# A two-layer hybrid block: the second layer's in-projection without the context columns of three query blocks

## The chip, the cores and the metric

One core of a Trainium2 chip runs the whole program in one launch. The metric is the device time of that launch in microseconds. Engines: TensorE (PE; its weight loads are PEld), VectorE (DVE), ScalarE (ACT), GpSimd (POOL), and SyncE (SP), which here issues all data transfers.

## What is computed

The reference runs two layers over 1024 latent tokens and 256 context tokens of width 1024. Each layer normalises and modulates the tokens, projects them into the columns of four mixers (two attentions, a state-space model, a long convolution called hyena), runs the mixers, gates them, and projects back. The second layer returns only latent tokens:

```python
for l in range(DEPTH):
    need_ctx = l < DEPTH - 1
    p_l = h_l @ w_in[l]
    p_c = h_c @ w_in[l]
    a_l, a_c = mla_mixer(p_l[..., :o1], p_c[..., :o1], ..., need_ctx)
    g_l, g_c = gqa_mixer(p_l[..., o1:o2], p_c[..., o1:o2], ..., need_ctx)
```

In both attentions the context tokens give keys and values in either layer, `k_c, v_c = keys(p_ctx, False)`. They give queries only where `need_ctx` holds: `o_c = attend(p_ctx, k_c, v_c, False) if need_ctx else None`. So in the second layer the query columns of the context tokens are read by nothing.

## The kernel before

The normalised tokens of a layer lie in SBUF as `hh` and `hl`, the high and low parts of 8 tiles of 128 features by 1280 tokens (1024 latent, then 256 context). The in-projection goes by blocks of 128 output columns. `inproj_cols` (L468) loads a block's weights as `wraw`, splits them into `whi` (ACT, L459) and `wlo` (POOL), and goes over the tokens in chunks: the first of 512, the next of `step`. A chunk is 24 matmuls into one PSUM tile `ipc`: 8 feature tiles, each as `hh` by `whi`, `hl` by `whi` and `hh` by `wlo` (`mm3`, recorded at L224). A `sink` then takes the chunk out of PSUM.

`inproj_qkv` (L492) does this for the seven blocks of the attentions, always over 1280 tokens. Blocks 0 and 1 are the queries of the grouped attention, 2 its keys, 3 its values. Block 4 and the lower half of block 6 are the compressed queries of the latent attention, block 5 its compressed keys and values, and the upper half of block 6 the rotary key. Blocks other than 3 have an entry in `SUMS` (L490): for them the sink also squares the chunk (`sq`), and after the second and the third chunk PE multiplies the squares with a selector `bsel`, 128 tokens at a time. DVE copies these sums of squares into the tile `rs` (128 tokens by 10 token tiles by 8 columns; L518). Block 6 adds its own to those of block 4 there. With `step` 384 the chunks of such a block are 512, 384 and 384.

`prep` (L1384) turns the projected blocks into queries, keys and values in DRAM, in five chunks of 256 tokens, the last the context. It begins with `rs`: DVE adds `eps`, POOL raises the 128x80 tile to the power -1/2 (L1414, tile `nhalf`), DVE negates it into `nrs`. For each chunk it loads `px` and `py` from `qkvD`, transposes `rs` (`prt`), spreads it (`pbc`), rotates (`pR`), and multiplies up (`mv`, `mkn`, `mqn`, `mqr`). `need_q` is false for the context chunk of the second layer.

A layer's program order is in the table `SCRIPT` (L1819). For the second layer it is `Whhuuhqqqqqqqhhh`: W builds the hyena filters (`hps`, `hfilt`, `fdft`, `kt`) and the state-space tables (`pwt`, `sT`, `sF`, `etp`, `kfp`), h projects a hyena block, u a state-space block, q an attention block. After it come, at high priority, hyena (`hyx`, `ldft`, `lX`, `dd`, `ds`, `lU`, `lout`), the state-space scans (`sU`, `sD`, `sV`, `cm`), `prep`, and the finishing stage `ssm_finish` (L1317; `sgy`, `sgg`, `sz`, `sglu`). Then come the projections of the eight gate blocks (`inproj_gate`, `ipt`), attention (`aq`, `kst`, `aS`) and the output projection. The instruction order on each engine is set by a scheduler at build time, from priorities and its own estimate of durations; each engine then runs its queue in order.

Of the kernel before, what the change touches and what calls it, by code (L numbers as in the profile page):

```python
# [187 lines left out]
class K:  # L188
# [300 lines left out]

    SUMS = {0: (128, 0, 2, 0), 1: (128, 0, 2, 2), 2: (128, 2, 2, 4), 4: (128, 4, 1, 6), 6: (64, 4, 1, 6), 5: (128, 5, 1, 7)}  # L490

    def inproj_qkv(self, l, blk, P):  # L492

        late = []

        def sink(ps, c0, m):
            o = P.tile([128, 512], F32, tag="ipo", name="ipo", bufs=3)
            self.nc.scalar.copy(o[:, :m], ps[:, :m])
            self.store(self.qkvD[:, blk, c0:c0 + m], o[:, :m])
            if blk not in self.SUMS:  # L500
                return
            r, s, k, d = self.SUMS[blk]
            sq = P.tile([128, 512], F32, tag="ipo", name="sq", bufs=3)
            self.act(sq[:r, :m], ps[:r, :m], AF.Square)
            late.extend((sq, t) for t in range(m // 128))
            if m == 512:
                return
            nt = len(late)
            q = ps[:, 384:384 + nt * k].rearrange("p (t k) -> p t k", k=k)
            for i, (sq, t) in enumerate(late):  # L510
                self.mm(q[:, i], sq[:r, t * 128:t * 128 + 128], self.bsel[:r, s:s + k], i == 0, i == nt - 1)
            late.clear()
            i1 = (c0 + m) // 128
            dst = self.rs[:, i1 - nt:i1, d:d + k]
            if blk == 6:
                self.tt(dst, q, dst, ADD)
            else:
                self.nc.vector.tensor_copy(dst, q)  # L518

        self.inproj_cols(self.A["w_qkv"][l, blk], 1280, sink, 384 if blk in self.SUMS else 512)  # L520

    def inproj_gate(self, l, g, n, P):

# [860 lines left out]
    def prep(self, l, W, nq):  # L1384


        nc, A = self.nc, self.A
# [29 lines left out]
        for c0, n in self.CHUNKS:  # L1417
            c = slice(c0, c0 + n)
            i0, nt = c0 // 128, n // 128
            lat, need_q = c0 < 1024, c0 < nq  # L1420
            p0 = 0 if need_q else 2
            x = W.tile([128, 7, 256], F32, tag="px", name="px")
            self.load(x[:, p0:6], self.qkvD[:, p0:6, c])
            if need_q:
                for h in range(2):
                    self.load(x[h * 64:h * 64 + 64, 6], self.qkvD[0:64, 6, c])
# [377 lines left out]
def weave(*gens):  # L1804

    out = [None] * len(gens)
    live = dict(enumerate(gens))
    while live:
        for i, g in list(live.items()):
            try:  # L1810
                next(g)
            except StopIteration as e:
                out[i] = e.value
                del live[i]
    return out
# [7 lines left out]
def dit_kernel(ctx: ExitStack, tc: tile.TileContext, A, out):  # L1823
    k = K(tc, A, out)
    k.setup(ctx)
    nc = tc.nc
# [3 lines left out]
    for l in range(2):  # L1830
        need = l == 0
        n = 1280 if need else 1024
# [17 lines left out]
        with k.pool("fil", side="right") as F, k.pool("pol") as Q:  # L1850
            fil = k.filters(l, F, need)
            next(fil)
            mr = ExitStack()
            if l == 0:
                M = mr.enter_context(k.pool("mod"))
                with tc.high_priority(20000):
                    k.mod_setup(M)
                    scl, shf = k.modulation(0, M)
            with k.pool("polt") as P, tc.high_priority(20000):
                poles = k.ssm_poles(l, P, Q)  # L1860
            if l == 0:
                with tc.high_priority(20000), k.pool("np") as P:
                    for g0 in range(0, 10, 2):
                        xns = []
                        for i in (g0, g0 + 1):
                            xt = P.tile([128, 1024], F32, tag="xt", name="xt", bufs=2)
                            k.load_x(xt, i)
                            xn = P.tile([128, 1024], F32, tag="xn", name="xn", bufs=3)
                            k.xn_tile(P, xt, xn, xn)
                            xns.append(xn)  # L1870
                        k.norm_cols(P, (g0, g0 + 1), xns, scl, shf, k.hh, k.hl, 3)
            mr.close()
            tr = ExitStack()
            gens = {"f": fil, "t": k.ssm_tables(l, tr.enter_context(k.pool("tab")), poles)}
            done = {}
            k.rs = k.cp.tile([128, 10, 8], F32, tag="rs", name="rs")

            def step(c):
                if c in done:
                    return False  # L1880
                try:
                    next(gens[c])
                except StopIteration as e:
                    done[c] = e.value
                    tr.close() if c == "t" else None
                return True

            def scan():
                with k.pool("ssm") as Q:
                    weave(k.ssm(l, Q, uD, yD, done["t"], need))  # L1890

            blocks = dict.fromkeys("uqh", 0)
            for c in SCRIPT[l]:
                if c in blocks:
                    x = blocks[c]
                    blocks[c] += 1
                if c == "u":
                    k.inproj_raw(A["w_col"][l, x], 1280, uD[:, x], k.wp)
                elif c == "q":
                    k.inproj_qkv(l, x, k.wp)  # L1900
                elif c == "h":
                    k.inproj_raw(A["w_col"][l, 2 + x], n, hyD[:, x], k.wp)
                elif c in "ft":
                    step(c)
                elif c in "FT":
                    while step(c.lower()):
                        pass
                elif c == "W":
                    while step("f") | step("t"):
                        pass  # L1910
            kf = done["f"]
# [94 lines left out]
```

## Time and profile before

| | |
|---|---|
| median of 3 runs | 2175.04 us (2175.00, 2175.04, 2179.42) |
| the profiled execution | 2180.56 us, its span 2178.8 us |
| mean granted TensorE clock | 0.932 |
| PE, PEld, DVE busy | 89%, 74%, 73% |
| ACT, POOL busy | 42%, 46% |
| second layer: first projection matmul | 1218.22 us |
| second layer: first attention scores | 1789.41 us |

The span is counted from the first to the last instruction, and what lies around it is 1.76 us. Busy shares are averages over stages: the second layer's in-projection, with the filters, scans and preparation woven into it, fills 1218 to about 1790 us, attention 1790 to about 2060, the output projection the rest.

### The profile page before, as it was taken

How to read it: one execution, taken by the hardware profiler on the slowest of the kernel's cores; microseconds unless marked ns; L12 is line 12 of the kernel's file. 1: busy time of each engine (PE TensorE's matmuls, PEld its weight loads, DVE VectorE, ACT ScalarE, POOL GpSimd, SP SyncE). 2: the span in 40 equal slices, each digit the busy share in tenths (PEclk: the TensorE clock that was granted, in tenths of full speed). 3: DMA queues.
4: the chain of work that ended last, by engine and by line, in shares of the span. 5: the costliest groups of instructions: out<-in, count | busy, mean ns of one | idle time of the engine just before them, and what ended most of it. 6: DMA issues, size and time to landing. Idle time of an engine off the chain costs nothing.

```text
span 2178.8 us, 31556 instructions
## 1 busy us (share of the span) xinstructions
PE 1941.8 (89%) x10811; PEld 1615.2 (74%) x10811; DVE 1591.4 (73%) x2985; ACT 917.5 (42%) x1958; POOL 1000.7 (46%) x798
## 2 busy tenths in 40 slices
PE   5788998789899899999998898988888989999988
PEld 1577788678677777788776777888766667899866
DVE  7799528963986588788644398479768878999821
ACT  4422224223333376677523322334223227788611
POOL 4756325664752144434156549236565624240033
PEclk8698898999999999999899998999899999999999
DMA  6422455345766545553243433364456675561063
GB/s 205 133 79 105 148 169 163 102 121 176 228 194 211 170 124 139 161 141 96 80 153 116 129 108 120 125 225 143 129 160 204 209 219 145 141 168 55 11 184 125
DMA packets 261279, 316.55 MB, mean 145 GB/s; under 512 B 46670, under 2 KB 203598, under 8 KB 257792
## 3 DMA queue, kind: packets, MB, share of 16 engines
q1 hardware_dynamic: 261120, 314.55, 47.4%
q8 instruction: 85, 1.39, 0.3%
q14 instruction: 74, 0.61, 0.1%
HBM read 207.61 MB, written 106.86 MB: 144 GB/s over the span
## 4 chain that ended last, share of the span: by engine, by line
PE 44%; DVE 29%; DMA 10%; issue 7%; POOL 4%; ACT 3%; SPq 2%; POOLq 0%; DVEq 0%; ACTq 0%
PE ipc L224 8%; PE apo L224 7%; PE ops L224 6%; PE apt L253 6%; PE aS L224 6%; DVE lU L233 3%; DVE sD L233 3%; SPq L201 2%; DVE sp L233 2%; PE acx L224 2%; PE fdft L224 2%; PE mps L224 1%; DVE lX L233 1%; PE hps L224 1%; DMA px<-qkvD 1%
## 5 line engine op out<-in xcount | busy, mean ns | idle before, releaser
L224 PE MATMUL ipc<-hh,whi 128*128 128x512 f32 (+2 forms) x992 | 386.9, 390 | 24.3 <-DVE rs L518 9.6
L224 PE MATMUL ipc<-hh,wlo 128*128 128x512 f32 (+2 forms) x992 | 380.9, 384 | 3.5 <-POOL wlo L233 3.5
L224 PE MATMUL ipc<-hl,whi 128*128 128x512 f32 (+2 forms) x992 | 381.9, 385 | 1.6 <-POOL hl L233 1.6
L224 PEld LDWEIGHTS ipc<-hh,whi 128*128 128x128 f32 x992 | 196.8, 198 | 59.5 <-DVE rs L518 11.2
L1669 ACT CAST aPh<-apt 128x512 fp32r<-128x512 f32 x328 | 186.6, 590 | 124.3 <-PE apt L253 115.7
L233 DVE TENSOR_TENSOR aPl<-apt,aPh 128x512 fp32r<-128x512 f32 x328 | 223.8, 683 | 20.2 <-ACT aPh L1669 16.0
L233 POOL TENSOR_TENSOR wlo<-wraw,whi 128x512 fp32r<-128x512 f32 x108 | 164.3, 1527 | 154.6 <-ACT whi L459 144.0
L224 PEld LDWEIGHTS ipc<-hh,wlo 128*128 128x128 f32 x992 | 196.5, 198 | 34.8 <-POOL wlo L233 4.3
L224 PEld LDWEIGHTS ipc<-hl,whi 128*128 128x128 f32 x992 | 197.0, 199 | 32.9 <-issue 3.6
L253 PE MATMUL apt<-ident,aP 128*128 128x128 f32 x1312 | 190.0, 275 | 1.5 <-DVE aPl L233 1.0
L1634 DVE TENSOR_REDUCE am<-aS 128x1 f32<-128x1024 f32 x128 | 155.5, 1215 | 13.5 <-PE aS L224 13.5
L224 PE MATMUL aS<-kst,aq 128*128 128x512 f32 x512 | 153.3, 422 | 11.7 <-DMA aq<-gP 6.8
L246 ACT ACTIVATE aP<-aS,am,rs 128x1024 f32<-128x1024 f32 x128 | 155.7, 1217 | 15.3 <-DVE am L243 14.2
L253 PEld LDWEIGHTS apt<-ident,aP 128*128 128x128 f32 x1312 | 148.1, 140 | 16.8 <-DVE aPl L233 6.9
L1697 POOL COPY aLB<-am 128x128 f32<-128x128 f32 x72 | 21.2, 294 | 299.6 <-DVE am L1689 294.0
L224 PE MATMUL apo<-aPh,vst 128*128 128x256 f32 x656 | 138.0, 307 | 15.6 <-ACT aPh L1669 9.1
L224 PE MATMUL apo<-aPl,vst 128*128 128x256 f32 x656 | 123.3, 285 | 3.1 <-DVE aPl L233 3.1
L224 PEld LDWEIGHTS apo<-aPh,vst 128*128 128x128 f32 x656 | 96.0, 190 | 31.0 <-DVE aob L233 15.9
L459 ACT CAST whi<-wraw 128x512 fp32r<-128x512 f32 x124 | 75.5, 618 | 92.7 <-PE ipc L224 48.9
L224 PE MATMUL ops<-owh,omh 128*128 128x512 f32 x288 | 94.2, 408 | 16.4 <-ACT omh L1782 10.3
L224 PEld LDWEIGHTS aS<-kst,aq 128*128 128x128 f32 x512 | 88.7, 193 | 26.8 <-ACT aP L246 7.4
L224 PEld LDWEIGHTS apo<-aPl,vst 128*128 128x128 f32 x656 | 100.1, 189 | 10.0 <-DVE aPl L233 5.3
(368 smaller groups left out, 4490.4 us busy)
## 6 DMA issues: line engine op xcount, KB each, us to landing
wraw<-in_w_col_dram SPq DMA_DIRECT2D x64, 256.0 KB
mraw<-in_w_mod_dram SPq DMA_DIRECT2D x32, 512.0 KB
kst<-mK SPq DMA_DIRECT2D x16, 640.0 KB
omx<-mixD SPq DMA_DIRECT2D x18, 512.0 KB
ogt<-gD SPq DMA_DIRECT2D x18, 512.0 KB
wraw<-in_w_mod_dram SPq DMA_DIRECT2D x32, 256.0 KB
k<-kt SPq DMA_DIRECT2D x16, 512.0 KB
lk<-k SPq DMA_DIRECT2D x8, 1024.0 KB
```

Source lines behind the costliest of these rows:

```text
L201: return self.nc.sync.dma_start(out=out, in_=in_)
L224: self.keep(self.nc.tensor.matmul(out, lhsT, rhs, start=start, stop=stop))
L233: self.keep((eng or self.nc.vector).tensor_tensor(out=out, in0=a, in1=b, op=op))
L246: self.keep(self.nc.scalar.activation(out=out, in_=in_, func=func, **k))
L253: self.keep(self.nc.tensor.transpose(out, in_, self.ident[:p, :p]))
L459: self.nc.scalar.copy(hi, raw)
L1634: self.keep(nc.vector.tensor_reduce(out=x["m"][:, 2 + qi:3 + qi], in_=x["S"][qi], axis=AX.X, op=ALU.max))
L1669: self.keep(nc.scalar.copy(h, ps))
L1697: self.keep(nc.gpsimd.tensor_copy(x["LB"][:, :, o:o + 64], x["m"][:, 10:12].unsqueeze(2).to_broadcast([128, 2, 64])))
```

## The change

`inproj_qkv` is given the layer's number of token columns `n` (1280 in the first layer, 1024 in the second) and uses it for blocks 0, 1 and 4. In the second layer these are projected over the 1024 latent tokens, in chunks of 512, 256 and 256. Blocks 2, 3, 5 and 6 keep 1280 tokens. The context entries of `rs` that the three blocks no longer fill are set by a memset to 1.0 ahead of the projection. `prep` loads the context chunk's `px` in two pieces, without block 4. The first layer's code stays as it was.

```diff
-    def inproj_qkv(self, l, blk, P):
+    def inproj_qkv(self, l, blk, n, P):
         late = []
+        n = n if blk in (0, 1, 4) else 1280
...
-        self.inproj_cols(self.A["w_qkv"][l, blk], 1280, sink, 384 if blk in self.SUMS else 512)
+        self.inproj_cols(self.A["w_qkv"][l, blk], n, sink, (384 if n == 1280 else 256) if blk in self.SUMS else 512)
...
             x = W.tile([128, 7, 256], F32, tag="px", name="px")
-            self.load(x[:, p0:6], self.qkvD[:, p0:6, c])
+            for p in (slice(0, 6),) if need_q else (slice(2, 4), slice(5, 6)):
+                self.load(x[:, p], self.qkvD[:, p, c])
...
             k.rs = k.cp.tile([128, 10, 8], F32, tag="rs", name="rs")
+            if not need:
+                nc.vector.memset(k.rs, 1.0)
...
-                    k.inproj_qkv(l, x, k.wp)
+                    k.inproj_qkv(l, x, n, k.wp)
```

The scheduler orders the second layer anew with these sizes. Three places of the new order matter here.

On PE, from hyena's `lout` transforms to the last sums of squares of block 6 (`ldft` are hyena's next transforms, `gv` the first work of prep; between the rows stand projection matmuls). Before:

```order
L224 MATMUL lout<-lX,hfi 128x128 x12
...
L224 MATMUL ldft<-hyt,hff 128x128 x8
L224 MATMUL ipc<-bsel,sq 128x1 x7
...
L224 MATMUL ipc<-hl,whi 128x384
L224 MATMUL ipc<-hh,whi 128x512
...
L224 MATMUL ipc<-bsel,sq 128x1 x3
L253 MATMUL gv<-ident,px 128x128 x2
```

Now:

```order
L224 MATMUL lout<-lX,hfi 128x128 x12
...
L224 MATMUL ipc<-hh,wlo 128x384
L224 MATMUL ldft<-hyt,hff 128x128 x8
L224 MATMUL ipc<-hh,whi 128x512
...
L224 MATMUL ipc<-bsel,sq 128x1 x2
L224 MATMUL ldft<-hyt,hff 128x128 x8
L224 MATMUL ipc<-bsel,sq 128x1
L224 MATMUL ipc<-hl,whi 128x512
```

Between `lout` and the last `bsel` there stood 26 projection matmuls of 384 columns and 24 of 512; now there are 4 and 16.

On DVE, the adds of block 6's sums into `rs`, the add of `eps`, and what of hyena and prep stands around them. Before:

```order
L233 TENSOR_TENSOR hyt<-lout,hyt 128x512 x2
L233 TENSOR_TENSOR rs<-ipc,rs 128x7
L233 TENSOR_TENSOR ds<-lX 128x1024
L233 TENSOR_TENSOR lX<-ds 128x2x256 x2
L233 TENSOR_TENSOR lU<-lX 128x2x128 x4
L233 TENSOR_TENSOR sp<-px,sp 128x256 x2
...
L236 SCALAR_TENSOR_TENSOR py<-py,gqk,prg 128x256 x2
L233 TENSOR_TENSOR rs<-ipc,rs 128x3
L233 TENSOR_TENSOR rs<-rs,eps 128x80
...
L241 TENSOR_SCALAR nrs<-rs 128x80
```

Now:

```order
L233 TENSOR_TENSOR hyt<-lout,hyt 128x512 x2
L233 TENSOR_TENSOR rs<-ipc,rs 128x7
L233 TENSOR_TENSOR rs<-ipc,rs 128x3
L233 TENSOR_TENSOR rs<-rs,eps 128x80
L233 TENSOR_TENSOR ds<-lX 128x1024
L233 TENSOR_TENSOR lX<-ds 128x2x256 x2
L233 TENSOR_TENSOR lU<-lX 128x2x128 x4
L233 TENSOR_TENSOR sp<-px,sp 128x256 x2
...
L236 SCALAR_TENSOR_TENSOR py<-py,gqk,prg 128x256 x2
L241 TENSOR_SCALAR nrs<-rs 128x80
```

The second add and the `eps` add have moved from behind `py` to ahead of `ds`.

On POOL, the power of `rs` (`rs<-rs,nhalf`), with hyena's `dd`, `lX`, `lU` and `ds` and prep's weight splits `uq`, `ukvl`. Before:

```order
L233 TENSOR_TENSOR dd<-lX 128x1024
L233 TENSOR_TENSOR uq0l<-swr,uq0h 128x512
L233 TENSOR_TENSOR wlo<-wraw,whi 128x512
L233 TENSOR_TENSOR lX<-dd 128x2x128 x4
...
L233 TENSOR_TENSOR lU<-lX 128x2x128
L233 TENSOR_TENSOR rs<-rs,nhalf 128x80
...
L233 TENSOR_TENSOR lX<-lX 128x2x128
...
L233 TENSOR_TENSOR ds<-lU,lk 128x1024
```

Now:

```order
L233 TENSOR_TENSOR dd<-lX 128x1024
L233 TENSOR_TENSOR rs<-rs,nhalf 128x80
L233 TENSOR_TENSOR uq0l<-swr,uq0h 128x512
...
L233 TENSOR_TENSOR lX<-dd 128x2x128 x4
L233 TENSOR_TENSOR wlo<-wraw,whi 128x512
...
L233 TENSOR_TENSOR lU<-lX 128x2x128
...
L233 TENSOR_TENSOR lX<-lX 128x2x128
...
L233 TENSOR_TENSOR ds<-lU,lk 128x1024
```

The power has moved from behind hyena's first `lU` to right behind `dd`, ahead of `uq0l` and `lX`.

## Rows read from the trace of the kernel before

**Rows 1.** The page's table of busy time (share of the span), instructions.

```profile
PE 1941.8 (89%) x10811; PEld 1615.2 (74%) x10811; DVE 1591.4 (73%) x2985; ACT 917.5 (42%) x1958; POOL 1000.7 (46%) x798
```

**Rows 2.** Windows: length; busy PE, PEld, DVE, ACT, POOL; PE clock; DMA share; GB/s.

```profile
1320.00:1340.00 20.00, 19.02 (x88) 15.71 (x89) 16.68 (x22) 3.28 (x6) 18.77 (x11) 0.66 0.30 111
...
1380.00:1400.00 20.00, 20.00 (x141) 17.48 (x140) 11.26 (x34) 6.72 (x18) 3.33 (x3) 1.00 0.20 79
1400.00:1420.00 20.00, 20.00 (x154) 19.12 (x153) 5.37 (x21) 6.87 (x16) 4.95 (x6) 1.00 0.43 113
...
1500.00:1520.00 20.00, 13.87 (x63) 12.94 (x62) 19.88 (x24) 4.30 (x12) 15.97 (x14) 0.74 0.27 86
```

**Rows 3.** The chain that ended last, end of the filters: start, us, what.

```profile
1414.15 7.14 PE fdft L224 x64
1421.69 5.28 DMA k<-kt
```

**Rows 4.** Timeline of PE, end of the attention blocks: start, us, instruction.

```profile
1547.56 3.03 PE L224 MATMUL lout<-lX,hfi 128*128 128x128 f32 x24
...
1557.62 1.95 PE L224 MATMUL ldft<-hyt,hff 128*128 128x128 f32 x16
...
1566.34 0.83 PE L224 MATMUL ipc<-bsel,sq 64*128 64x1 f32 x6
```

**Rows 5.** Timeline of POOL around the power of `rs`.

```profile
1560.27 3.46 POOL L233 TENSOR_TENSOR dd<-lX 128x1024 f32<-128x1024 f32 x1 [5.12 <-ACT lX L803]
1563.69 1.29 POOL L233 TENSOR_TENSOR uq0l<-swr,uq0h 128x512 fp32r<-128x512 f32 x1
...
1566.63 3.81 POOL L233 TENSOR_TENSOR lX<-dd 128x256 f32<-128x256 f32 x4
...
1576.51 0.73 POOL L233 TENSOR_TENSOR lU<-lX 128x256 f32<-128x256 f32 x1
1577.20 13.16 POOL L233 TENSOR_TENSOR rs<-rs,nhalf 128x80 f32<-128x80 f32 x1
...
1594.21 2.42 POOL L233 TENSOR_TENSOR ds<-lU,lk 128x1024 f32<-128x1024 f32 x1 [0.69 <-DVE lU L236]
```

**Rows 6.** Timeline of DVE there; in brackets idle time and what ended it.

```profile
1560.23 1.23 DVE L233 TENSOR_TENSOR ds<-lX 128x1024 f32<-128x1024 f32 x1 [3.05 <-ACT lX L803]
...
1575.88 0.15 DVE L233 TENSOR_TENSOR rs<-ipc,rs 128x3 f32<-128x3 f32 x1
1576.07 0.58 DVE L233 TENSOR_TENSOR rs<-rs,eps 128x80 f32<-128x80 f32 x1
...
1590.39 1.26 DVE L241 TENSOR_SCALAR nrs<-rs 128x80 f32<-128x80 f32 x1 [12.10 <-POOL rs L233]
```

**Rows 7.** Windows, one from preparation to attention, columns as in rows 2.

```profile
1600.00:1800.00 200.00, 167.62 (x786) 128.69 (x785) 162.46 (x240) 62.86 (x145) 100.21 (x77) 0.93 0.71 214
```

**Rows 8.** Timeline of PE: first and last of 71, 24 and 38 projection matmuls.

```profile
1237.94 0.39 PE L224 MATMUL ipc<-hl,whi 128*128 128x512 f32 x1
...
1254.20 0.40 PE L224 MATMUL ipc<-hh,wlo 128*128 128x512 f32 x1
...
1260.88 0.28 PE L224 MATMUL ipc<-hh,whi 128*128 128x256 f32 x1
...
1263.61 0.28 PE L224 MATMUL ipc<-hh,wlo 128*128 128x256 f32 x1
...
1427.78 0.34 PE L224 MATMUL ipc<-hh,wlo 128*128 128x384 f32 x1
...
1434.29 0.34 PE L224 MATMUL ipc<-hh,whi 128*128 128x384 f32 x1
```

**Rows 9.** Timeline of SP's queue: the issue of one of prep's loads.

```profile
1651.89 0.62 SPq L201 DMA_DIRECT2D px<-qkvD  x1
```

**Rows 10.** Timeline of PE, the finishing stage ahead of attention.

```profile
1785.62 3.75 PE L224 MATMUL sglu<-sz,sgw 128*128 128x256 f32 x8 [3.83 <-ACT ipt L246]
...
1795.91 3.78 PE L224 MATMUL sglu<-sz,sgw 128*128 128x256 f32 x8 [4.45 <-DVE sz L236]
```

## The prediction

> **What bounds the kernel now.** I read the page's table of engines first [rows 1]. TensorE (PE) is busy 89% of the span and VectorE (DVE) 73%, which alone says only that neither can be ignored. The edit lies in layer 1's in-projection, so next come the windows of that stretch [rows 2]. Before 1340 us both engines are loaded. From 1380 to 1420 PE is busy 20.00 of 20 us at full granted clock while DVE is busy 11.26 and 5.37: there PE alone sets the pace, and the chain of work that ended last runs through it, ending in 7.14 us of filter transforms and the DMA `k<-kt` behind them [rows 3]. From 1500 to 1520 it is the other way round: DVE 19.88 of 20, PE 13.87 at a granted clock of 0.74. Removing columns pays in the first kind of window and not in the second.
>
> The third place to see is the hinge from in-projection to attention preparation. The last sums of squares end on PE at about 1567 [rows 4]. DVE adds them only at 1575.88, because it runs in order and first does hyena work and the rotary products. GpSimd (POOL) then takes 13.16 us for the power -1/2 of the 128x80 tile `rs`, from 1577.20 to 1590.36 [rows 5], and DVE idles 12.10 us for it at `nrs` [rows 6]. After that, from 1600 to 1800, DVE is busy 162.46 of 200 us, 0.81 [rows 7]; nothing there is saturated, but every dependent step has to get through DVE's queue.
>
> **The change, part by part.**
> *Columns.* Blocks 0, 1 and 4 go from chunks 512+384+384 to 512+256+256. The number of matmuls stays; 48 per block lose 128 columns each, 144 in all. Steady spacing, start to start [rows 8]: 512 columns (1254.20-1237.94)/70 = 0.232 us, 384 columns (1434.29-1427.78)/37 = 0.176, 256 columns (1263.61-1260.88)/23 = 0.119. So each saves 0.057 us, a block 2.7 us, all three 8.2 us of PE time at full clock. The spacing is proportional to columns, about 0.46 ns a column: the weight loads hide even behind 256. The Trainium skill (TensorE: Matmul & The Clock Gate, Back-to-back issue gap) says that in streams of load and matmul pairs the spacing is 81 ns at 128 columns and 131 at 512, set by both operations. By an estimate from that page, 128 columns would be worth 17 ns and the change 2.4 us of PE time in place of 8.2; the rows of this kernel differ, and they decide.
>
> *Blocks 0 and 1* stand on PE ahead of the filter transforms. By the order, the transforms that end at 1421 had 96 chunks' matmuls of 384 columns and 72 of 512 before them since the same point of the queue, and now have 96 of 256 and 80 of 512. That is 96 x 0.057 = 5.5 us less and 8 x 0.232 = 1.9 us more, 3.6 us net at best. Half of the saving (block 0, 2.7 us) falls before 1350, where DVE is loaded too (16.68 of 20 us busy while PE has 19.02 [rows 2]), so I count half of that: 5.5 - 1.35 - 1.9 = **2.2 us** earlier, bounds 0 and 3.6.
>
> *Block 4's* 2.7 us lie in the stretch where DVE is full. I count nothing for them there, since PE's idle time behind DVE covers them; without that cover they would be worth their 2.7 us. They only let the projection run ahead of the scans, which leads to the next term.
>
> *The hinge.* In the new order, between the start of hyena's `lout` transforms and the last sums PE has 4 projection matmuls of 384 columns and 16 of 512, where before it had 26 and 24. That is 22 x 0.176 + 8 x 0.232 = 5.7 us less. The last sums, at 1566.34 + 0.83 = 1567.2 [rows 4], would end at 1561.5. DVE's queue has moved as well: both adds and the eps add now stand right behind `hyt`, ahead of `ds`, `lX`, `lU` and the rotary products. So `rs` is ready about 0.7 us after the sums, at 1562.2. POOL's queue has the power right behind `dd`, which ends at 1560.27 + 3.46 = 1563.7 [rows 5]. The power then starts at 1563.7, not 1577.2: **13.5 us** earlier, and prep's first chunk with it.
>
> What of this is kept? Hyena does not gain: in POOL's new order `uq0l`, the four `lX` and the rest that ran from 1563.69 to 1577.20 now come behind the power, so hyena's `ds`, at 1594.21 before, stays about where it was (13.5 earlier, 13.5 more ahead of it). What is regained is DVE's idle time: the 12.10 us wait at `nrs` is now filled by `ds` to `py`, which took from 1560.23 to 1575.88 [rows 6]. They start at 1562.2 rather than 1560.23 (1.9 us lost, waiting for the sums) and end near 1576, and the power ends at 1576.9, so about 1 us of wait is left. 12.1 - 1.9 - 1.0 = 9.2 us of DVE time. In the stretch that must absorb it DVE is 0.81 busy [rows 7], so I count 9.2 x 0.81 = **7.5 us**. Bounds: 0 if attention waits for hyena alone, 13.5 if it waits for prep alone. I take a value between, nearer to the row of DVE's idle time, since both chains share DVE.
>
> *Small parts.* A 128x80 memset of `rs` is added on DVE, early in layer 1, long before the first sums: between 0.1 us and the 0.58 us of the eps add of the same shape [rows 6], hidden while the filters run. The context chunk's load becomes two DMAs for one: one more issue, 0.62 us of the SP queue for such a load [rows 9], with its chunk long projected. Evictions, squares and stores of 12 chunks shrink on ACT, which is 42% busy [rows 1]: nothing. Fewer sums: 8 tiles for 10 in three blocks, inside the numbers above.
>
> *The tail.* Before, `sglu` of the finishing state-space stage waited 3.83 us for a gate's `ipt` and 4.45 us for `sz` [rows 10]. In the new order all gates' matmuls stand ahead of the last `lout`. The first wait may go (gain up to 4 us), or the gates may hold up `lout`, with the same price the other way. I take 0.
>
> **Sum:** 2.2 + 7.5 = 9.7 us. The profiled execution took 2180.56 us, so 2170.9 for its like; the median of the runs shown is 2175.04, 5.5 us below that execution, so 2165.3 as the prediction. The three runs lie within 4.4 us, and 0.2% (4.35 us) is about what a measurement of this kernel can tell from no change.
>
> **The rivals.**
> *Hidden.* The end is set by hyena on DVE, whose work does not change, and prep's head start is lost again among its waits. For it: DVE full before 1540, and hyena's `ds` not moving in my own sum. Against: the 12.10 us in which DVE stands idle cannot survive the new order. The gain is then 0 to 4 us; with half of the 2.2 us, 2174. Chance 0.19. The Trainium skill (Perfetto Trace Analysis, Identifying the Most-Contended Engine) warns that matmul busy time is a poor measure of TensorE's load and gives weight-load busy time instead. That page would lean to this rival, and here weight loading is busy 74% [rows 1]; the full windows between 1380 and 1420 with matmuls back to back are the evidence against it.
>
> *Slower: hyena behind the power.* The power's new place in POOL's queue delays `lX`, `lU` and `ds` of hyena by those 13.5 us of moved work. It breaks even only if the power starts 13.5 us earlier. If the last sums are late on PE (the second `ldft`, which waits for `hyt`, stands ahead of the last of them), each microsecond missing there comes onto hyena. Should the power gain under 7 us, hyena ends 6.5 us later, less 2.2: 4.3 us slower, past 0.2%. If it gains nothing, 13.5 - 2.2 = 11.3 us, 2186. For it: POOL is in order and hyena's last transforms are among the last things before attention. Against: 5.7 us less stands ahead of the sums. Chance 0.13.
>
> *PE sets everything.* If PE is what attention waits for, the whole 8.2 us count, and stalls like the 3.83 us of [rows 10] and the freed hinge may add as much again: 2158. Chance 0.10, on the faster side.
>
> *The change does nothing:* excluded, since the order has the rows of 256 columns.
>
> **How the numbers follow.** My forecast, a gain of 4.4 to 16 us, has 0.58; with the PE rival that makes 0.68 for faster by over 0.2%. Hidden, 0.19, is the case within 0.2%. Slower has 0.13. The range: the top gain of the bounds 3.6 + 13.5 + 4 = 21 us gives 2154, and I set 2153. At the top it takes in the hidden case and small losses, to 2178. Left out are the worse half of the slower rival and gains beyond the bounds, under 2 in 10.
>
> **What would show it.** In the new profile: projection matmuls of 256 columns at 0.119 us spacing in three blocks; `k<-kt` issued 0 to 4 us earlier; the 128x80 power starting near 1562 (13 to 16 us earlier) with its 13 us unchanged; the wait of `nrs` down from 12.1 to under 4 us; hyena's first `ds` on POOL near 1592 to 1595; attention's first scores 5 to 15 us earlier; from there to the end no change. I am wrong if the power starts later than about 1570, if hyena's `ds` comes later than before, or if prep starts earlier and the first scores do not.

## The result, and the profile after

The changed kernel takes 2189.43 us (median of 4 runs, 2187.36 to 2193.12) against 2175.43 us: a ratio of 1.0060, 95% interval 1.0045 to 1.0076. It is 0.6% slower, where 0.45% faster was predicted; the profiled execution took 2193.12 us.

Two traces have to be set on a common event before their times are compared. Layer 0 is the same in both programs, and its last store is this row of SP's queue, in the kernel before and then in the changed one, and there with the store `k<-kt` that answers to [rows 3] (start, us, instruction):

```profile
1222.58 0.33 SPq L201 DMA_DIRECT2D xD<-oy  x1
```

```profile
1215.78 0.33 SPq L201 DMA_DIRECT2D xD<-oy  x1
...
1416.45 0.54 SPq L201 DMA_DIRECT2D k<-kt  x1
```

By the plain times `k<-kt` comes 5.2 us earlier than in [rows 3]. But layer 0 had taken 6.8 us less in this execution. From the seam it is 1421.69 - 1222.58 = 199.1 us before and 1416.45 - 1215.78 = 200.7 after: 1.6 us *later*. All times "from the seam" below are counted like this.

PE, around the second half of the first long convolution and in the second half's first one (answers to [rows 4]; in brackets idle time and what ended it):

```profile
1550.27 2.84 PE L224 MATMUL lout<-lX,hfi 128*128 128x128 f32 x24
...
1561.42 2.05 PE L224 MATMUL ldft<-hyt,hff 128*128 128x128 f32 x16
...
1626.38 1.22 PE L224 MATMUL lout<-hfi,lX 128*128 128x128 f32 x4 [4.14 <-DVE lX L233]
...
1637.55 2.84 PE L224 MATMUL lout<-hfi,lX 128*128 128x128 f32 x24
```

POOL and then DVE there, for [rows 5] and [rows 6]:

```profile
1564.17 2.42 POOL L233 TENSOR_TENSOR dd<-lX 128x1024 f32<-128x1024 f32 x1 [6.87 <-ACT lX L805]
1566.55 14.14 POOL L233 TENSOR_TENSOR rs<-rs,nhalf 128x80 f32<-128x80 f32 x1
...
1599.11 2.41 POOL L233 TENSOR_TENSOR ds<-lU,lk 128x1024 f32<-128x1024 f32 x1 [0.70 <-DVE lU L236]
```

```profile
1552.03 0.69 DVE L233 TENSOR_TENSOR hyt<-lout,hyt 128x512 f32<-128x512 f32 x1 [4.38 <-PE lout L224]
...
1563.89 0.16 DVE L233 TENSOR_TENSOR rs<-ipc,rs 128x3 f32<-128x3 f32 x1 [9.06 <-PE ipc L224]
1564.09 0.24 DVE L233 TENSOR_TENSOR rs<-rs,eps 128x80 f32<-128x80 f32 x1
...
1580.72 1.29 DVE L241 TENSOR_SCALAR nrs<-rs 128x80 f32<-128x80 f32 x1 [3.51 <-POOL rs L233]
```

The wait at `nrs` went from 12.10 to 3.51 us, as foreseen. From the seam, however, the power starts at 350.8 against 354.6 us, 3.9 earlier and not 13.5. Hyena, which was to stay where it was, is late: its first `hyt` comes at 336.3 us against 326.9, the second `dd<-lX` at 348.4 against 337.7, `ds` behind the power at 383.3 against 371.6. It never makes that up.

The page's table and two windows (columns as in [rows 1] and [rows 2]):

```profile
PE 1941.6 (89%) x10799; PEld 1618.2 (74%) x10799; DVE 1592.2 (73%) x2986; ACT 915.9 (42%) x1958; POOL 983.0 (45%) x798
```

```profile
1600.00:1800.00 200.00, 161.34 (x758) 126.03 (x756) 155.47 (x232) 60.65 (x137) 99.04 (x76) 0.88 0.67 201
...
1780.00:1820.00 40.00, 18.52 (x69) 13.55 (x69) 21.70 (x34) 12.95 (x29) 7.11 (x4) 0.66 0.72 191
```

PE is busy as long as before with less to do: between 1600 and 1800 it works 161 of 200 us and not 168 as in [rows 7], at a granted clock of 0.88 and not 0.93. From 1780 to 1820 no projection is left, PE waits for the finishing stage, and the granted clock is 0.66. (These two windows go by plain times.) The stage's last two matmul groups (for [rows 10]) wait 8.68 and 9.14 us, where they waited 3.83 and 4.45:

```profile
1790.18 3.78 PE L224 MATMUL sglu<-sz,sgw 128*128 128x256 f32 x8 [8.68 <-DVE sz L236]
...
1807.08 3.78 PE L224 MATMUL sglu<-sz,sgw 128*128 128x256 f32 x8 [9.14 <-DVE sz L236]
```

From the seam the last `sglu` starts at 591.3 us against 573.3, and from there to the end of the span it is 384 us against 383.

### The profile page after: what moved, and what is told of

It is laid out like the page before. It is cut to its first block, busy times and chain, and to the rows that moved or that the text cites. A ratio compares the mean times of both kernels' runs of the same rounds, so it can differ in the third digit from the quotient of the medians.

```text
span 2191.3 us, 31529 instructions
## 1 busy us (share of the span) xinstructions
PE 1941.6 (89%) x10799; PEld 1618.2 (74%) x10799; DVE 1592.2 (73%) x2986; ACT 915.9 (42%) x1958; POOL 983.0 (45%) x798
## 4 chain that ended last, share of the span: by engine, by line
PE 45%; DVE 30%; DMA 8%; issue 7%; POOL 5%; ACT 2%; SPq 2%; POOLq 0%; DVEq 0%; ACTq 0%
PE ipc L224 9%; PE apo L224 7%; PE ops L224 6%; PE apt L253 6%; PE aS L224 6%; DVE sD L233 3%; DVE lU L233 3%; SPq L201 2%; PE acx L224 2%; PE fdft L224 2%; DVE sp L233 1%; DVE lX L233 1%; PE mps L224 1%; PE lout L224 1%; PE hps L224 1%
## 5 line engine op out<-in xcount | busy, mean ns | idle before, releaser
L233 POOL TENSOR_TENSOR wlo<-wraw,whi 128x512 fp32r<-128x512 f32 x108 | 156.1, 1450 | 166.2 <-ACT whi L459 160.5
```

Of the source, the lines that this page charges most:

```text
L233: self.keep((eng or self.nc.vector).tensor_tensor(out=out, in0=a, in1=b, op=op))
```

## The experiments

The expectations name these theories by letters:

- **A**: the power's new place on POOL delays hyena.
- **B**: hyena's `lout` and `ldft` stand behind projection on PE.
- **C**: the cut columns, the memset or the split load cost by themselves.
- **D**, **F**, **G**: the finishing stage is what attention waits for. By D POOL's conversions slow it, by F it needs a fixed time behind hyena and its own first load, by G most of the loss arises in it.
- **E**: the columns save nothing, since PE only runs dry where DVE sets the pace.
- **H**: the loss is the whole order into which the scheduler put the five queues.

Each time is the median of 5 to 12 runs, with its ratio to the kernel before, timed beside it, and a 95% interval.

### Parts of the change, and the power

e2_b01, blocks 0 and 1 alone:

```diff
-        n = n if blk in (0, 1, 4) else 1280
+        n = n if blk in (0, 1) else 1280
```

> The change for blocks 0 and 1 alone; block 4 keeps its 1280 columns. The order then puts the power on POOL behind hyena's four lX and lU<-lX again, as in the kernel before (in the changed kernel it stands ahead of them), while the filters end as early as in the changed kernel (k<-kt near 1416). Theory A (the power's place on POOL delays hyena, and the end waits for hyena): hyena's ds on POOL no later than 1594, and 2166 to 2175 us, 0 to 9 faster than before. Theory B (hyena's lout and ldft stand behind projection matmuls on PE, whatever POOL does): here the lout follow after 58 to 63 us of projection against 55 to 63 in the changed kernel, so the loss stays, 2182 to 2190. Theory C (256-column chunks or the added memset and split load cost by themselves): two of three blocks, so two thirds of the 14 us, about 2185.

Measured: 2187.70 us, ratio 1.0052 (1.0040 to 1.0065). The power stands behind `lU` again, and it is still slow: against A. The place of the loss has changed too: from the seam the last `hyt` ends at 545.9 us as before, but the last `sglu` starts 36.1 us behind it and not 27.4.

e3_b4, block 4 alone (`if blk == 4`):

> The change for block 4 alone; blocks 0 and 1 keep 1280 columns. The order has the power on POOL ahead of hyena's four lX, as in the changed kernel, and the filters end as late as before (k<-kt near 1421). Theory A: the power holds hyena up as in the changed kernel and the filters' gain is missing: 2185 to 2195 us, 10 to 20 slower than before. Theory B: the second half's first lout stands behind 62.5 to 64 us of projection after the filters, 1 more than before: 2176 to 2182. Theory C: one of three blocks, a third of the 14 us, about 2180.

Measured: 2182.97 us, 1.0034 (1.0023 to 1.0044), between the theories. The parts don't add up to the whole (0.52 + 0.34 against 0.60%); each has an order of its own.

e4_pieces, the power by chunks, behind hyena's `lX` and `lU` on POOL:

```diff
-        self.tt(self.rs, self.rs, self.nhalf[:, 0:8].unsqueeze(1).to_broadcast([128, 10, 8]), ALU.pow, nc.gpsimd)
-        self.ts(self.nrs, self.rs, -1.0)
...
+            r = self.rs[:, i0:i0 + nt]
+            self.tt(r, r, self.nhalf[:, 0:8].unsqueeze(1).to_broadcast([128, nt, 8]), ALU.pow, nc.gpsimd)
+            self.ts(self.nrs[:, i0:i0 + nt], r, -1.0)
```

> The changed kernel with the power taken in five pieces of 128x16, one in each chunk of attention preparation, and nrs with it. The order puts all five in one row on POOL, but behind hyena's four lX and lU<-lX, where the kernel before has the power. Theory A: hyena's ds on POOL no later than 1594, and 2166 to 2177 us. Theory B: PE's queue has the first half's lout behind 55 to 62 us of projection as in the changed kernel, so 2183 to 2190. Theory C: all three blocks have 256-column chunks, 2189 as the changed kernel.

Measured: 2191.33 us, 1.0067 (1.0053 to 1.0082). Against A once more.

e6_sqrt and e7_bsqrt, the power off POOL in the changed kernel and in the kernel before:

```diff
-        self.tt(self.rs, self.rs, self.nhalf[:, 0:8].unsqueeze(1).to_broadcast([128, 10, 8]), ALU.pow, nc.gpsimd)
+        self.act(self.rs, self.rs, AF.Sqrt)
+        nc.vector.reciprocal(self.rs, self.rs)
```

> The changed kernel with the power -1/2 of the 128x80 tile taken off POOL: a square root on ACT and a reciprocal on DVE give the same values. PE's order is that of the changed kernel up to the second half's first ldft, and differs behind them. Theory A: without the 13 to 14 us of the power on POOL hyena's ds comes near 1585, and the time falls under the kernel before: 2155 to 2172 us. Theory B: hyena stays behind the projection on PE: 2183 to 2190, as lout and ldft of that place do not move in the order. Theory C: 2189. Which share of the 14 us goes says how much of the loss is the power's.

> The kernel before with the power off POOL (a square root on ACT, a reciprocal on DVE). PE's order up to the second half's ldft is that of the kernel before. If the power's 13 us on POOL are on the path that sets the end (Theory A), 5 to 12 us faster than before, 2163 to 2170. If hyena then only waits behind projection on PE, or the end does not wait for hyena: 2173 to 2177.

Measured: 2178.16 us, 1.0019 (1.0003 to 1.0034), and 2164.80 us, 0.9953 (0.9939 to 0.9967). DVE in e7_bsqrt, and the `ds` that follows on POOL:

```profile
1573.39 0.65 DVE L1415 RECIPROCAL rs<-rs 128x80 f32<-128x80 f32 x1 [0.34 <-ACT rs L246]
1574.08 0.20 DVE L241 TENSOR_SCALAR nrs<-rs 128x80 f32<-128x80 f32 x1
```

```profile
1578.50 2.41 POOL L233 TENSOR_TENSOR ds<-lU,lk 128x1024 f32<-128x1024 f32 x1 [0.69 <-DVE lU L236]
```

With the seam at 1219.35, `ds` comes at 359.2 us, 12.4 earlier than before. The power is on the path, in both kernels, and the kernels without it are faster by 11.3 and 9.8 us. (From hyena's second half on the scheduler ordered these two anew as well, and how much of the gain is that order was not separated.) So the power isn't what tells the kernels apart: without it they are still 13.4 us from each other. A falls. e7_bsqrt beats both kernels.

### Hyena behind the gates, and the tail

f1_edges holds the gates behind hyena's later `lout`:

```diff
         for g in range(8):
-            k.inproj_gate(l, g, n, k.wp)
+            j = {1: 1, 2: 1, 3: 1, 4: 2, 5: 2, 6: 2, 7: 3}.get(g) if l else None
+            with tc.issue_after(k.marks[j]) if j is not None else nullcontext():
+                k.inproj_gate(l, g, n, k.wp)
```

> The changed kernel with the gate projections held behind hyena in PE's queue: gates 1 to 7 are queued behind the last matmul of the second, third and fourth lout (1 to 3, 4 to 6, 7). Everything up to the second half's ldft keeps the changed kernel's order, the power's early place on POOL too. The three lout then follow after 109, 143 and 176 us of projection since the filters, in the changed kernel 120, 160 and 188, before 109, 148 and 181. Theory B (hyena behind projection on PE): hyena's last hyt comes 6 to 10 us earlier than in the changed kernel and the time falls to 2177 to 2183. Theory A (the power on POOL): the delay stands already at hyena's ds, so 2186 to 2191. Theory D (the end waits for the finishing stage and for what slows it, not for hyena): hyena earlier, the time within 3 us of 2189.

Measured: 2180.01 us, 1.0027 (1.0012 to 1.0041), 9.4 us under the changed kernel, and the intervals don't overlap. The second half's first `lout` on PE:

```profile
1628.51 4.36 PE L224 MATMUL lout<-hfi,lX 128*128 128x128 f32 x24 [0.72 <-DVE lX L237]
```

It starts at 1628.51, while DVE writes the last `lX` (the last ends at 1629.12). In the changed kernel the last `lX` was there at 1632.4, and `lout` started at 1637.55, 5 us later, behind 22 projection matmuls of 512 columns. B holds for this part of the path.

f4_modlate, and f5_edgemod with f1's edit as well (`fin` is the finishing stage's last `sth`):

```diff
-            nc.gpsimd.tensor_copy(hi, raw)
-            self.lo(lo, raw, hi, nc.gpsimd)
+            with self.tc.issue_after(self.fin) if l else nullcontext():
+                nc.gpsimd.tensor_copy(hi, raw)
+                self.lo(lo, raw, hi, nc.gpsimd)
```

> The changed kernel with one thing moved: POOL's conversions of the modulation weights (mhi, mlo) start only once the finishing stage's last sth is there. The order of every other engine is that of the changed kernel. In the changed kernel's trace DVE's last four operations of the finishing stage took 7.3 us beside them, where the same operations take 1.6 us elsewhere. Theory D (the finishing stage, slowed by POOL's conversions, is what attention waits for): these 5.7 us come back, 2182 to 2186. Theories A and B alone, with a tail that costs nothing: 2188 to 2191.

> Both of the last two edits together in the changed kernel: gates behind hyena's lout on PE, modulation conversions behind the finishing stage on POOL. If hyena behind projection and the slowed finishing stage are the two parts of the loss, their gains add: 2171 to 2179. If one hides the other: no lower than the better of the two alone.

Measured: 2186.66 us, 1.0050 (1.0031 to 1.0069), and 2180.44 us, 1.0025 (1.0011 to 1.0038). The stage's last operations on DVE, with POOL's beside them, in the changed kernel, and then DVE's in f4_modlate:

```profile
1799.88 1.14 DVE L233 TENSOR_TENSOR sgg<-sgg,sgy 128x256 f32<-128x256 f32 x1
1800.94 1.12 DVE L243 TENSOR_SCALAR sgg<-sgg 128x256 f32<-128x256 f32 x1
1802.10 2.44 DVE L233 TENSOR_TENSOR sgg<-sgg,sgy 128x256 f32<-128x256 f32 x1
1804.47 2.89 DVE L236 SCALAR_TENSOR_TENSOR sz<-sgg,sgy 128x256 f32<-128x256 f32 x2
...
1799.59 2.33 POOL L332 CAST mhi<-mraw 128x1024 fp32r<-128x1024 f32 x2 [33.17 <-DMA mraw<-in_w_mod_dram]
1801.89 4.85 POOL L233 TENSOR_TENSOR mlo<-mraw,mhi 128x1024 fp32r<-128x1024 f32 x2
```

```profile
1797.04 0.42 DVE L233 TENSOR_TENSOR sgg<-sgg,sgy 128x256 f32<-128x256 f32 x1
1797.38 0.29 DVE L243 TENSOR_SCALAR sgg<-sgg 128x256 f32<-128x256 f32 x1
1797.70 0.42 DVE L233 TENSOR_TENSOR sgg<-sgg,sgy 128x256 f32<-128x256 f32 x1
1798.04 0.99 DVE L236 SCALAR_TENSOR_TENSOR sz<-sgg,sgy 128x256 f32<-128x256 f32 x2
```

7.6 us against 2.1 for the same four rows. The stretch is real, but the time gained by 2.8 us only, with intervals that overlap, between the two forecasts of f4; and f5 is not below f1. Whether one hides the other, as the expectation has it, or the stretch costs next to nothing, these runs do not tell.

### Holding back the first half too

g1_first adds, to f1's edit, that the projection's last chunks queue behind hyena's first half; g3_bfirst is the kernel before with the same holds, g2_sqrtfirst and g4_bsqrtfirst have the power off POOL besides:

```diff
+                        for chunks, ins in ((k.chunks[-8:], k.marks[0]), (k.chunks[-7:], k.dfts[-3])):
+                            for i in sum(chunks, []):
+                                tc.add_manual_dep(i, ins.name, mybir.DependencyInfo(
+                                    mybir.DependencyClass.NoSync, mybir.DependencyReason.DATA), reason="behind")
```

> The changed kernel with the gates held behind hyena as in f1_edges, and besides the last blocks of the projection held behind hyena's first half: the second and third chunk of the last query block, and the three blocks behind it, are queued on PE behind the last matmul of the first lout, and the third chunk and those blocks also behind the second ldft. The first lout then follows after 55 us of projection since the filters (changed kernel 55 to 63, before 61 to 64), the second ldft after 59 (64 to 68, before 67); the power comes back behind hyena's lU<-lX on POOL. Theory B (the whole loss is hyena behind projection on PE): 2166 to 2176. Then, if the 8 us of columns are saved in truth, 2164 to 2170; if they only leave PE dry where DVE sets the pace (Theory E), level with before, 2171 to 2177. If something else in the change costs (Theory C): 2178 or more.

> The same holds in the changed kernel, and the power off POOL (a square root on ACT, a reciprocal on DVE). Theory B with the columns saved: 2155 to 2162, under the 2164.8 of the kernel before without the power. Theory E (no saving arrives): 2162 to 2168. Theory C: 2170 or more.

> The same holds in the kernel before, as a control: its first lout moves from behind 61 to 64 us of projection to behind 60, its second ldft from 67 to 64, the later lout by at most 2 us. Theory B: hyena gains 1 to 3 us at most, 2171 to 2177. Should this be faster by 5 us or more, then the holds help by themselves and g1_first says less about the change.

> The same holds in the kernel before with the power off POOL, the control for g2_sqrtfirst. Theory B: 2158 to 2166, near the 2164.8 without the holds. The difference to g2_sqrtfirst is what the cut columns are worth when hyena isn't held up: 4 to 8 us if they are saved in truth, under 2 by Theory E.

Measured: g1 2195.62 us, 1.0090 (1.0076 to 1.0105); g2 2178.99, 1.0020 (1.0007 to 1.0033); g3 2178.10, 1.0012 (1.0001 to 1.0023); g4 2177.34, 1.0011 (0.9997 to 1.0025). B as I had it falls: against their like without holds g1 lost 15.6 us, g4 12.5, g3 2 and g2 1. Preparation's first transposes on PE in g1_first, and in f1_edges:

```profile
1599.41 0.38 PE L256 MATMUL prt<-ident,rs 128*8 128x128 f32 x2
```

```profile
1580.19 0.38 PE L254 MATMUL prt<-ident,rs 128*8 128x128 f32 x2
```

What is held back feeds the sums, the power and preparation. From the seam hyena ends at 553.2 us in g1 (554.2 in f1), but preparation starts 18 us later, the finishing stage makes its first load at 546.2 and not at 530.5, and the time is longer by about as much. That hyena and preparation both hold up that stage is argued from this pair, not shown, and g2 is against it as a rule: there preparation starts 16 us later than in e6 (367.7 against 351.9) and the first load comes 12 us later, at a cost of 0.8 us.

### Clearing the finishing stage

k1_tail has f4's edit, and the weights' loads behind the stage's last load (`fld`) on SP; k6_b01tail, k3_sqrtedgetail and k4_bsqrttail are e2, e6 with f1's edit, and e7, with the same:

```diff
-                self.load(t, src)
+                with self.tc.issue_after(self.fld) if self.fld else nullcontext():
+                    self.load(t, src)
```

> The changed kernel with the finishing stage cleared of what runs into it: the loads of output and modulation weights (owr, mraw) are queued on SP behind the stage's last load, and POOL's conversions of the modulation weights behind its last sth. PE's order is that of the changed kernel. Theory F (the end is set by the finishing stage, which needs about 37 us from its first load and 23 from hyena's last store): with hyena still late, 2183 to 2187, as f4_modlate (2186.7), since the weights' loads lie ahead of it. Theory G (the tail itself holds most of the loss): 2175 to 2181.

> e2_b01 (blocks 0 and 1 alone cut) with the same clearing of the finishing stage. In the trace of e2_b01 hyena ended as early as before, counted from the end of the first layer, and preparation too, but the stage's last loads, with modulation and output weights and attention's loads around them, landed 7 us late and the stage took 46 us in place of 38. Theories F and G: the loss of e2_b01, 12 us, falls to 2 to 6, so 2177 to 2182. If the loss arises earlier: 2185 to 2189.

> The changed kernel with all that was found to help: the power off POOL, gates held behind hyena's lout, and the clearing of the finishing stage. If the cut columns are worth their PE time once nothing holds hyena or the finishing stage up: 2152 to 2160, 5 us or more under k4_bsqrttail. If PE only runs dry where DVE sets the pace (Theory E): level with k4_bsqrttail or up to 6 slower, 2160 to 2170.

> The kernel before with the power off POOL and the clearing of the finishing stage; no gates held, since hyena's lout already follow after 104, 146 and 181 us there. Control for k3_sqrtedgetail. In e7_bsqrt's trace the stage took 37 us, about its least, so 2161 to 2166, at most 4 under e7_bsqrt.

Measured: k1 2184.34 us, 1.0041 (1.0025 to 1.0057); k6 2184.03, 1.0036 (1.0022 to 1.0051); k3 2179.20, 1.0015 (0.9997 to 1.0033); k4 2166.69, 0.9960 (0.9946 to 0.9974). By the medians the tail is worth 5 us in k1, within F's forecast, and 4 in k6, between its two forecasts, both with intervals that overlap. In k4 it is worth nothing, and k3, which has f1's edit besides, is no faster than e6 without either (2178.16). That is against G. And k3 to k4 is the telling pair: with every single cause that I had found taken away (k4 holds no gates back, since its `lout` already come as early as f1's), the kernel with fewer columns is still 12.5 us slower, and k3 is over all its forecasts.

### Each kernel in the other's order

o1_order is the changed kernel held to the order of the kernel before on all five engines, over the stretch in which the built programs differ (1706 instructions of PE, 573 of DVE, and so on); o2_border is the kernel before in the order of the changed one:

```diff
+    for e, runs in ORDER.items():
+        last = None
+        for r in runs.split():
+            a, n = map(int, (r + ":1").split(":")[:2])
+            for i in own[e][a:a + n]:
+                if last is not None:
+                    tc.add_manual_dep(i, last.name, mybir.DependencyInfo(
+                        mybir.DependencyClass.NoSync, mybir.DependencyReason.DATA), reason="order")
+                last = i
```

> The changed kernel, columns cut, in the order of the kernel before: over the stretch in which the two orders differ, every instruction of PE, DVE, ACT, POOL and the SP queue is held behind the one ahead of it there. Theory H (the loss is the order as a whole): no slower than before, 2168 to 2176; what it lies under 2175 is what the cut columns are worth, at most 8 us, and 0 to 3 if PE only runs dry where DVE sets the pace. Theory C (the cut columns, the memset or the split load cost by themselves): 2182 to 2190.

> The kernel before, no column cut, in the order of the changed kernel on all five engines. Theory H: slower than before by the loss of the order, as slow as the changed kernel or up to 8 us slower still, 2187 to 2197. Theory C: the order is harmless, 2173 to 2178.

Measured: o1 2174.14 us, 0.9990 (0.9977 to 1.0004); o2 2193.43 us, 1.0084 (1.0066 to 1.0103). That settles the cause, which is the order taken as a whole:

| ratio to before | order of before | order of the change |
|---|---|---|
| all columns | 1 | 1.0084 |
| columns cut | 0.9990 | 1.0060 |

The order costs 0.70 to 0.84%, 15 to 18 us. The columns give back 0.10 to 0.24%, 2 to 5 us, and in the old order not more than can be told from nothing. H holds, C falls, and E is near the truth. No run held a kernel to its own order. Should the holds cost something by themselves, then the table shows the cut columns too small in the old order and too large in the new one, and the order's price too small with the columns cut and too large without. The means, 0.17% for the columns and 0.77% for the order, are free of that. Page and PE in o1_order, the latter the first and last of 20 projection matmuls of 256 columns, and a wait that follows:

```profile
PE 1934.0 (89%) x10799; PEld 1607.3 (74%) x10799; DVE 1601.7 (74%) x2986; ACT 914.8 (42%) x1958; POOL 998.3 (46%) x798
```

```profile
1339.70 0.28 PE L224 MATMUL ipc<-hl,whi 128*128 128x256 f32 x1
...
1341.95 0.28 PE L224 MATMUL ipc<-hh,wlo 128*128 128x256 f32 x1
...
1345.31 1.05 PE L224 MATMUL sps<-ones,hacc 128*128 128x1 f32 x8 [1.92 <-POOL hacc L233]
```

The spacing is 2.25 / 19 = 0.118 us, and PE is busy 7.8 us less than in [rows 1]: the work is gone as computed, the time stays. From the seam (us):

| | before | o1 | after | o2 | f1 | e7 | e6 |
|---|---|---|---|---|---|---|---|
| `k<-kt` after the filters | 199.1 | 198.5 | 200.7 | 203.8 | 199.9 | 198.7 | 200.0 |
| first `hyt` | 326.9 | 326.7 | 336.3 | 340.2 | 333.1 | 326.6 | 333.1 |
| second `dd<-lX` | 337.7 | 337.5 | 348.4 | 352.3 | 345.3 | 337.3 | 345.2 |
| second `ds<-lU,lk` | 371.6 | 371.4 | 383.3 | 387.2 | 380.2 | 359.2 | 367.4 |
| third `dd<-lX` | 437.1 | 434.5 | 452.1 | 455.0 | 442.0 | 420.5 | 434.1 |
| last `hyt` ends | 545.9 | 543.9 | 561.1 | 564.6 | 554.2 | 534.1 | 547.6 |
| last `sglu` starts | 573.3 | 572.3 | 591.3 | 592.8 | 575.4 | 559.1 | 571.1 |

Every kernel in the change's order is 6 to 13 us behind at the first `hyt`, ahead of the power and of the late `lout`. One trace is one execution: six kernels with the same order up to there (the changed one, f1, f4, f5, e6, k1) reach it at 333.1 to 336.3 us, so 3 us between two columns may be chance. DVE ahead of that place in the changed kernel, and in o1_order:

```profile
1533.81 1.80 DVE L233 TENSOR_TENSOR lX<-lU 128x256 f32<-128x256 f32 x2
...
1537.39 1.73 DVE L233 TENSOR_TENSOR sD<-sV,cm 64x256 f32<-64x256 f32 x4
...
1540.62 1.53 DVE L1269 TENSOR_TENSOR_SCAN sV<-sR,sD 128x320 f32<-128x320 f32 x2
1542.07 1.80 DVE L236 SCALAR_TENSOR_TENSOR lX<-lX,lU 128x256 f32<-128x256 f32 x2
...
1545.13 1.73 DVE L233 TENSOR_TENSOR sD<-sV,cm 64x256 f32<-64x256 f32 x4
1546.89 0.76 DVE L236 SCALAR_TENSOR_TENSOR lX<-lU 128x256 f32<-128x256 f32 x2
```

```profile
1538.34 3.59 DVE L233 TENSOR_TENSOR lX<-lU 128x256 f32<-128x256 f32 x4
1541.85 1.02 DVE L233 TENSOR_TENSOR sV<-sV,stb 128x318 f32<-128x318 f32 x1
1542.80 1.73 DVE L233 TENSOR_TENSOR sD<-sV,cm 64x256 f32<-64x256 f32 x4
1544.56 0.42 DVE L236 SCALAR_TENSOR_TENSOR lX<-lX,lU 128x256 f32<-128x256 f32 x1
```

In the new order two rounds of the scan (`sV`, `sD`) stand in DVE's queue between hyena's `lX` rows, in the old one part of one. From the seam DVE's last `lX` ends at 331.9 us in the changed kernel and at 325.6 in the kernel before: 6.3 of the 9.4 us. The rest is PE's. Between the first 8 and the last 24 matmuls of this `lout` its queue has 44 projection matmuls of 384 columns, where 14 stood, and then the scan's `sy` and the sums; the wait for `lout` at `hyt` is 4.38 us against 1.36. The first of the 44 waits for DVE's copy of sums, which stands among the scan's rows:

```profile
1536.67 0.69 PE L224 MATMUL ipc<-hh,whi 128*128 128x384 f32 x1 [2.95 <-DVE rs L520]
```

After this wait the granted clock is 0.50 from 1536 to 1542, the lower of its two levels (1.2 GHz), and the matmuls of 384 columns are 0.32 us apart and not 0.176. That these rows are the dearest of the new order is a reading of traces; no run moved them alone.

## Why the prediction was wrong

- **Columns: right in size, wrong in worth.** They took 0.118 us a matmul, and 7.8 us of PE went, about as worked out. But in the old order they bring 2 us, which can't be told from nothing. The prediction's estimate of 2.4 us of PE, from the spacings in the Trainium skill (TensorE: Matmul & The Clock Gate, Back-to-back issue gap), does not agree with the trace.
- **Blocks 0 and 1, 2.2 us earlier: right in the old order, wrong in the new one, and read from the wrong row.** From the seam the last filter transform on PE starts at 198.3 us before, at 195.3 in o1_order and at 199.8 in the changed kernel: 3.0 us earlier, within the bounds, and 1.5 later. Of the 5.5 us of columns ahead of it a new wait for POOL's `hacc` takes 1.92 in o1_order; the discount was made for DVE alone, though [rows 2] have POOL at 18.77 of 20 us there. The store `k<-kt` shows little of this (199.1, 198.5, 200.7), because SP issues it straight behind a row of other transfers. At the first `hyt` of o1_order 0.2 of the 3.0 us are left; between the transforms and `lout` DVE was busy 117.9 of 126.3 us before, so the columns that went became idle time of PE.
- **Block 4 counted at nothing: right, as far as known.** With all three blocks cut the first `hyt` of o1_order moves 0.2 us; no run has block 4 alone in the old order.
- **The hinge, 7.5 us: the step that failed.** I took the new order of PE and POOL at this one place and kept everything ahead of it as it was in the old trace: `dd` ending at 1563.7, the second `ldft` in time. But from the seam `dd` is 10.7 us later, and the sums stand behind that `ldft`. So the power gained 3.9 us, not 13.5, and "hyena does not gain" was 11.7 us late at `ds`. The 5.7 us of projection that left the place between `lout` and the sums had not gone: they stand ahead of most of `lout` now. And I read DVE's new order for the adds, not for the rows of the scan between hyena's.
- **The wait at `nrs`, to about 1 us: nearly right** (3.51), and worth nothing: from the seam `nrs` comes 2.9 us earlier (364.9 against 367.8), and preparation's first transposes of `rs` on PE, which stand behind projection, start at 367.8 in both. The lower bound, "0 if attention waits for hyena alone", left out that hyena could itself be late.
- **The tail, 0 within 4: right for the stage, too small for the gates.** From the last `hyt` to the last `sglu` 27.4 us became 30.2; the two waits of [rows 10] grew because their data was late. But "the gates may hold up `lout`" came true, not at the last `lout`, which I looked at, but at the second half's first, 5 us behind its data; f1_edges, whose edit holds back the gates alone, is 9.4 us faster by the medians, more than the 4 allowed for.
- **The rival "hyena behind the power"** had the right side and victim, with the wrong cause. Between e6 and e7, with no power on POOL in either, `dd` is 7.9 us apart and the time 13.4; 10.7 of the 11.7 us at `ds` are there ahead of the power. That the power is waited for was in [rows 5] and [rows 6], but no reason for a difference.
- **"PE sets everything"** is refuted by o1; **"hidden"** is what the columns alone are. No rival was that the scheduler's new order is the worse as a whole, and it cost 15 to 18 us.

Open is why each part alone (e2, e3) falls on a poor order too, which of the new order's rows cost how much, and whether the cut columns in the old order with the power off POOL would beat e7_bsqrt: that wasn't tried.

## What to carry to other kernels

Where a scheduler sets the order, a change of a few sizes is two changes, the work and the order, and they are told apart by running each version in the other's order; here the order was worth several times the work. A wait that vanishes at one place is worth something only if the other chains that meet behind it come no later, so follow each of them through every in-order queue in the new order before counting the gain. Set two traces on a common event ahead of the change before reading a shift from them.

## What was not expected of the hardware

- The last store of the same layer 0 started between 1213.2 us (k1_tail) and 1224.2 us (e4_pieces) in the profiled executions. What sets this is open; it is as large as the effects sought.
- Beside POOL's conversion of 128x1024 tiles DVE's operations of 128x256 took 2.44 us and not 0.42 where they read two tiles, and 1.12 and not 0.29 where they read one. The Trainium skill (SBUF — State Buffer, SBUF: two separate sides) says that DVE and GpSimd share a pair of ports as an exclusive lock for a whole instruction, and that DVE needs it for operations with two SBUF inputs, when the GpSimd operation reads SBUF, or in a 2-port mode. The trace agrees in size: 2.44 us is about one of the two `mlo` (4.85 / 2), and the 1.12 us, like the 1.14 of the first row with two inputs, about one of the two `mhi` (2.33 / 2). Whether the row with one input ran in such a mode no run shows.
- The power of 80 elements a partition took 13.16 to 14.14 us on POOL. In e7_bsqrt the square root on ACT took 0.27 us in its place and the reciprocal on DVE 0.65.
